# Partition sums of three adaLN column groups by selector products and one transpose, with an opening product group, GpSimd's work and one seed moved

## The chip, the cores and the metric

The kernel runs on one core of a Trainium2 chip. The core has TensorE (PE in the profile; its weight loads are PEld), VectorE (DVE), ScalarE (ACT), GpSimd (POOL) and SyncE (SP), which here issues nearly all loads of weights. The metric is the time of one execution on the device in microseconds (us), the median of several runs.

## The reference

One decoder block on 256 tokens of width 2048, in fp32. A conditioning vector c gives, by one large matrix `w_ada` (2048 x 12288), a shift, a scale and a gate for each of two sub-layers; two convolutional or attention parts and a gated feed-forward net use them.

```python
mod = jax.nn.silu(c) @ w_ada[l] + b_ada[l]
sh1, sc1, g1, sh2, sc2, g2 = jnp.split(mod, 6, axis=-1)
h = modulate(rms_norm(x, norm1_g[l]), sh1, sc1)          # h * (1 + scale) + shift
q, k, v, gb, gc, xt = split(h @ w_in[l])                 # 6 x 1024 columns
mixed = concat(rms_norm(attention(rms_norm(q), rms_norm(k), v)), rms_norm(gb * causal_dwconv(gc * xt)))
x = x + g1 * (mixed @ w_out[l])
h2 = modulate(rms_norm(x, norm2_g[l]), sh2, sc2)
u_gate, u_up = split(causal_dwconv(h2 @ w_ffn_up[l]))    # 2 x 5632 columns
x = x + g2 * ((silu(u_gate) * u_up) @ w_ffn_down[l])
```

The six parts of `mod` are numbered 0 to 5 in the kernel; part 3 is the second shift and part 4 the second scale, each 2048 wide, as 16 chunks of 128 columns.

## The kernel before

**Main products.** Every weight matrix is read once, in pieces of 128 x 1024 fp32 (tile `raw`, 10 buffers, loaded by SP in one order). A piece is split in two: ACT rounds it to `hi` (fp32r, L947), and DVE or GpSimd subtracts to get `lo` (L958); there are 6 buffers of each. PE then makes three fp32r products for each block (L1194 to L1196): activations with `hi`, with `lo`, and the activations' own rest with `hi`; in the feed-forward part the same three stand as L1545 and L1549. The groups of in-projection products are called `mq`, `mk`, `mv`, `mg`, `mc`, `mx` by the columns that they make; their partial sums `pa_q`, `pa_k` and so on are taken out of PSUM by ACT (L1214) or added up by DVE (L1216), or put back as the start of the next group by ACT (a "seed"). `h0` to `h15` are the normed input's 16 chunks; each takes a subtraction on DVE or GpSimd (L1631).

**Slots.** The program is a list of some 205 slots of 24 main products each: 49 for the in-projection, 16 for the out-projection (names `m('A', f)` and `m('C', f)`), then the feed-forward part. In a slot ACT makes the `hi` and DVE or GpSimd the `lo` of the slot two further on. A table, `CFG`, says by hand which `lo` GpSimd makes (`'pool'`: 1 or 2 for one half of a slot, 3 for both, 0 for none), which partial sums are seeds, where each small step stands (`'move'`, `'cls'`), how many buffers there are and in what order the opening runs (`'start'`). Each engine works through its own list in order, so what waits holds back all behind it.

**adaLN.** A group of columns of `w_ada` (class `Ada`) is either multiplied on PE in tiles of 32 columns (L1034, the conditioning vector repeated 32 times, so that sums come out 32-fold), or by DVE, one row block at a time (L1049, L1051). Both leave a 128-row tile (`adae` or `ada`) whose column sums over the 128 partitions are wanted. `cols()` gets them: for each chunk of 128 columns a transpose on PE (L1089, tile `adac`), for each four chunks one sum by DVE (L1091, tile `adaz`), then two or one small DVE steps (L1099, L1104, L1105) into the columns A2 and B2, by which the second norm's output is scaled and shifted (L1435 `h2f`, L1440 `h`). The last `ada` step of a group on DVE that accumulates in PSUM writes to SBUF (`adae`) and so lets the bank go; banks are handed out in turn, and the next user waits.

**Opening.** Before slot 2 the list `'start'` mixes transposes of x (`xn`, tokens `tr`), their copies (`out`), first `ada` groups, and the first products (`go slot piece`). `xn7` is the last of the transposes.

**Attention.** `att_t` transposes (L1726), ACT copies `qT`, `kT` (L1729, L1730), `as` are the score products (L1737). L1755 is an ACT step on 128 x 128 fp32 there. The norm before the feed-forward part ends in `n2d` (DVE, L1412), a product `n2b`, and `rB` on ACT (L1419).

Of the kernel before, what the change touches and what calls it, by code (L numbers as in the profile page):

```python
# [14 lines left out]
P = 128  # L15
# [22 lines left out]
       'bufs': [41, 14, 10, 6, 2],  # L38
# [23 lines left out]
               18: 2,  # L62
# [57 lines left out]
               93: 2,  # L120
# [92 lines left out]
               64: 6,  # L213
# [7 lines left out]
               84: 1,  # L221
               90: 0,
# [13 lines left out]
               109: 4,  # L236
               159: 2,
# [19 lines left out]
                18: 2,  # L257
# [27 lines left out]
                58: 1,  # L285
# [6 lines left out]
                65: 1,  # L292
                66: 3,
                68: 2,
                72: 0,
                83: 0},
       'pool_h': [4, 5, 6, 7, 8, 9, 10, 11, 15],
# [57 lines left out]
                 67: 3,  # L355
                 69: 4,
# [112 lines left out]
                 'evac_in q1 True': 3,  # L469
# [48 lines left out]
                'att_o 2': (0, 2),  # L518
# [24 lines left out]
                'att_t 3': (0, -2),  # L543
# [5 lines left out]
                'broadcast 5 2': (-1, 0),  # L549
# [31 lines left out]
                'evac 1 8': (2, 0),  # L581
                'evac 2 4': (1, 3),
# [8 lines left out]
                'evac_c 3 1': (0, 1),  # L591
# [52 lines left out]
                'qk_stat q1': (4, -3),  # L644
# [16 lines left out]
                'up_conv 1': (-1, 0.5),  # L661
                'up_conv 14': (0, -1),
# [46 lines left out]
       'seed': ['c0 3', 'c1 3', 'k1 3', 'x0 1', 'k0 3', 'v0 2', 'g0 1', 'g1 2', 'g1 1', 'g0 2'],  # L709
# [9 lines left out]
       'conv': [[1, 2, 2, 5, 4, 7, 7, 8], [2, 3, 2, 3, 2, 3, 2, 6]],  # L719
# [3 lines left out]
       'fcols': 14,  # L723
# [11 lines left out]
       'fused': [2, 3, 7, 8, 9, 12, 13],  # L735
# [3 lines left out]
       'sq': [3, 6, 0],  # L739
       'tr': [4, 7, 1],  # L740
       'part': -1,
       'up': [[1, 3], [1, 3], [0, 0], [2, 2]],
       'gate': [-21, -14, -2, -11],
# [36 lines left out]
               'evac_out': 1},  # L780
# [3 lines left out]
       'hi_late': [1, 2, 3, 5, 7, 8, 9, 10, 13, 14, 15, 17, 19, 20, 21, 25, 26, 27, 32, 33, 34, 40, 49, 50, 51, 52, 55, 56,  # L784
# [6 lines left out]
def tile_block(  # L791
# [194 lines left out]
    class Ada:  # L986


        def __init__(self, part, c0, n, pe, psum=False):
            self.part, self.c0, self.n, self.pe, self.psum = part, c0, n, pe, psum or pe  # L990
            self.rows = 2048 // n
            self.tiles = NK // self.rows
            self.nch = n // P
            self.w = min(n, 512 if self.psum else n)
            self.seen = 0
            self.out = False
            self.own = [] if [part, c0] in CFG["own"] else None

# [20 lines left out]

        def consume(self, r, part=None):  # L1020
            if r == 0 and part != 1:
                self.start()
            if part != 0:
                self.seen += 1
            size = 1024 if self.own is None else 512
            for j in range(self.rows) if part is None else range(8 * part, 8 * part + 8):
                i = self.rows * r + j
                x = j * self.n % size
                if x == 0:
                    h = take() if self.own is None else self.own.pop(0)  # L1030
                t, last = h[:, x:x + self.n], self.own is None and x + self.n == 1024
                if self.pe:
                    q = 32 * (j % 4)
                    mm(self.acc[0][q:q + 32, :], crep[:, i, :], t,  # L1034
                       start=(r == 0 and j < 4), stop=(r == self.tiles - 1 and j >= self.rows - 4),
                       tile_position=(0, q))
# [40 lines left out]
        def cols(self):  # L1077
# [3 lines left out]
            for a in range(0, self.nch, 4):  # L1081
# [10 lines left out]
                self.finish(z, self.c0 + a, m, scale)  # L1092

# [639 lines left out]
    def att_s(h):  # L1733
# [261 lines left out]
    def slot(i):  # L1995
# [22 lines left out]
        for g, r in extra.get(i, []):  # L2018
            g.consume(r)
# [107 lines left out]
```

## Time and profile before

| what | value |
|---|---|
| median of 3 runs | 1174.56 us (1174.26 to 1174.75) |
| profiled execution | 1173.49 us |
| its span (first to last instruction) | 1171.6 us |
| granted TensorE clock | 0.998 |
| PE busy | 1155.4 us, 99% |
| DVE / ACT / GpSimd busy | 917.6 / 646.9 / 169.3 us |
| read from memory | 314.87 MB, 272 GB/s over the span |

The profile is one execution. A row of a timeline has the start and length in us, the engine, the line, the instruction, its output and inputs with shape, a count where several alike follow each other, and in brackets the time that the engine stood idle before it and what ended that. A row of the chain of waits has start, length and what the end of the program was waiting for in that time. A row of the groups by line has busy time, mean ns of one, and idle time. A wait for several things is put down to the one that came last by the profile.

### The profile page before, as it was taken

The page shows a single profiled execution, that of the slowest core. Times are in us where ns is not written, and L with a number is a line of the kernel's source. Part 1 is how long each engine was busy: PE and PEld are TensorE (multiplying, and loading weights), DVE is VectorE, ACT ScalarE, POOL GpSimd, SP SyncE. Part 2 cuts the span into 40 slices and gives each one's busy share as a digit, 9 for nine tenths or more (in the row PEclk, how much of TensorE's full clock was granted, in tenths as well). Part 3 has the DMA queues.
Part 4 walks back from the last instruction along what each step waited for, and adds up shares of the span by engine and source line. Part 5 has one row for each costly group of instructions (what it writes and reads, how often), then busy time and mean ns, then how long its engine had stood idle before and what let it go on. Part 6 is the DMA issues. An engine that isn't in the chain of part 4 may idle for free.

```text
span 1171.6 us, 17108 instructions
## 1 busy us (share of the span) xinstructions
PE 1155.4 (99%) x5989; PEld 965.8 (82%) x5989; DVE 917.6 (78%) x1311; ACT 646.9 (55%) x1002; POOL 169.3 (14%) x100
## 2 busy tenths in 40 slices
PE   7999999999999999999999999999999999999998
PEld 5678888878777878888888888888888888888886
DVE  4469979997788989999999544768888897666785
ACT  4666565578566455556676444555435554445461
POOL 0768673631001021000000000000000000000000
PEclk9999999999999999999999999999999999999999
DMA  9999999995799989986465755576887877875541
GB/s 349 405 405 374 406 353 386 390 388 170 262 368 315 362 272 360 378 276 208 156 207 187 235 180 181 175 230 220 284 299 262 306 245 231 292 246 174 169 155 72
DMA packets 205382, 320.22 MB, mean 273 GB/s; under 512 B 13816, under 2 KB 112300, under 8 KB 205296
## 3 DMA queue, kind: packets, MB, share of 16 engines
q1 hardware_dynamic: 202336, 314.68, 77.2%
q10 hardware_dynamic: 2352, 4.22, 1.3%
q8 instruction: 47, 0.77, 0.3%
q14 instruction: 39, 0.32, 0.1%
q0 software_dynamic: 608, 0.23, 0.1%
HBM read 314.87 MB, written 4.21 MB: 272 GB/s over the span
## 4 chain that ended last, share of the span: by engine, by line
PE 91%; DMA 5%; DVE 3%; issue 1%; ACT 0%; POOL 0%; SPq 0%; DVEq 0%; POOLq 0%; ACTq 0%
PE z L1545 27%; PE z L1549 14%; DMA raw<-in_w_in_dram 2%; DMA raw<-in_w_ada_dram 2%; PE ada L1034 1%; PE mx L1194 1%; PE mx L1196 1%; PE mx L1195 1%; PE mk L1194 1%; DVE ada L1051 1%; PE mg L1194 1%; PE mg L1196 1%; PE mc L1194 1%; PE mq L1194 1%; PE mc L1196 1%; PE mg L1195 1%
## 5 line engine op out<-in xcount | busy, mean ns | idle before, releaser
L947 ACT ACTIVATE hi<-raw 128x1024 fp32r<-128x1024 f32 (+1 forms) x401 | 401.2, 1030 | 314.2 <-PE z L1545 92.9
L958 DVE TENSOR_TENSOR lo<-raw,hi 128x1024 fp32r<-128x1024 f32 x340 | 397.6, 1208 | 95.6 <-ACT hi L947 90.3
L1545 PE MATMUL z<-h,hi 128*128 128x512 f32 x1408 | 328.9, 390 | 0.0
L1545 PEld LDWEIGHTS z<-h,hi 128*128 128x128 f32 x1408 | 261.3, 188 | 52.6 <-DVE h L1440 0.3
L1051 DVE SCALAR_TENSOR_TENSOR ada<-raw,csil,ada 128x512 f32<-128x512 f32 (+2 forms) x215 | 189.0, 892 | 5.6 <-DMA raw<-in_w_ada_dram 2.0
L958 POOL TENSOR_TENSOR lo<-raw,hi 128x1024 fp32r<-128x1024 f32 x61 | 150.5, 2489 | 269.2 <-ACT hi L947 269.2
L1549 PEld LDWEIGHTS z<-h,lo 128*128 128x128 f32 x1408 | 174.8, 192 | 3.4
L1549 PE MATMUL z<-h,lo 128*128 128x256 f32 x1408 | 176.0, 283 | 0.0
L1110 POOL MEMSET gb<- 128x512 f32 x2 | 1.1, 526 | 491.8 <-DVE uy L1484 491.8
L1461 DVE TENSOR_TENSOR ub<-z,ub 128x256 f32<-128x256 f32 x120 | 43.8, 417 | 34.5 <-ACT ub L1458 34.4
L1458 ACT ACTIVATE ub<-z 128x256 f32<-128x256 f32 x120 | 39.7, 383 | 31.1 <-PE z L1545 31.0
L1477 ACT ACTIVATE uy<-ub,vcols 128x256 f32<-128x256 f32 x88 | 45.6, 593 | 6.8 <-DMA gr<-gs 6.7
L1482 DVE SCALAR_TENSOR_TENSOR uy<-ub,vcols,uy 128x255 f32<-128x255 f32 x88 | 42.1, 479 | 5.7 <-ACT uy L1477 5.6
L1484 DVE SCALAR_TENSOR_TENSOR uy<-ub,vcols,uy 128x254 f32<-128x254 f32 x88 | 42.5, 483 | 3.1
L1493 ACT ACTIVATE gh<-uy 128x512 fp32r<-128x512 f32 x22 | 13.9, 630 | 40.6 <-DVE uy L1491 40.6
L1487 ACT ACTIVATE uy<-uy 128x512 f32<-128x512 f32 x22 | 13.9, 633 | 37.2 <-DVE uy L1484 37.2
L1034 PE MATMUL ada<-raw,crep 128*32 128x512 f32 (+1 forms) x224 | 27.1, 525 | 3.2 <-DMA raw<-in_w_ada_dram 2.7
L1494 DVE TENSOR_TENSOR gl<-uy,gh 128x512 fp32r<-128x512 f32 x22 | 15.2, 693 | 17.9 <-ACT gh L1493 17.9
L1194 PE MATMUL mk<-hi,h 128*128 128x512 f32 x64 | 25.8, 403 | 0.0
L1194 PE MATMUL mq<-hi,h 128*128 128x512 f32 x64 | 25.3, 395 | 0.4 <-ACT pa_g L1214 0.4
L1194 PE MATMUL mg<-hi,h 128*128 128x512 f32 x64 | 25.7, 401 | 0.0
L1194 PE MATMUL mx<-hi,h 128*128 128x512 f32 x64 | 25.3, 396 | 0.0
(574 smaller groups left out, 1922.8 us busy)
## 6 DMA issues: line engine op xcount, KB each, us to landing
raw<-in_w_ada_dram SPq DMA_DIRECT2D x180, 512.0 KB, 6.8
raw<-in_w_ffn_up_dram SPq DMA_DIRECT2D x352, 256.0 KB, 4.7
raw<-in_w_in_dram SPq DMA_DIRECT2D x95, 512.0 KB, 7.1
raw<-in_w_ffn_down_dram SPq DMA_DIRECT2D x76, 512.0 KB, 4.7
raw<-in_w_out_dram SPq DMA_DIRECT2D x32, 512.0 KB, 6.1
raw<-in_w_ada_dram SPq DMA_DIRECT2D x24, 256.0 KB, 6.6
raw<-in_w_ffn_down_dram SPq DMA_DIRECT2D x24, 256.0 KB, 3.8
xr<-in_x_dram SPq DMA_DIRECT2D x4, 512.0 KB, 5.4
```

What stands on the lines that cost most here:

```text
L947: act(piece(his, "hi")[:, :m], t[:, :m], AF.Copy)
L958: (nc.gpsimd if pool in (i + 1, 3) else V).tensor_tensor(out=piece(los, "lo")[:, :m], in0=t[:, :m], in1=hi[:, :m].bitcast(F32), op=ALU.sub ...
L1034: mm(self.acc[0][q:q + 32, :], crep[:, i, :], t, start=(r == 0 and j < 4), stop=(r == self.tiles - 1 and j >= self.rows - 4), tile_positio ...
L1051: V.scalar_tensor_tensor(out=self.acc[n], in0=v, scalar=csil[:, i:i + 1], in1=acc, op0=ALU.mult, op1=ALU.add)
L1194: mm(o, a, hi[k], start=(first and k == 0 and not seeded), stop=False, skip_group_check=True)
L1458: act(c[ft // 2][:, (ft % 2) * 256:(ft % 2) * 256 + 256], zp[grp][ft][:, 256:], AF.Copy)
L1461: V.tensor_tensor(out=d, in0=zp[grp][ft][:, :256], in1=d, op=ALU.add)
L1477: act(y, b, AF.Identity, bias=fcols[3][:, i:i + 1], scale=fcols[2][:, i:i + 1])
L1482: V.scalar_tensor_tensor(out=y[:, 1:], in0=b[:, :255], scalar=fcols[1][:, i:i + 1], in1=y[:, 1:], op0=ALU.mult, op1=ALU.add)
L1484: V.scalar_tensor_tensor(out=y[:, 2:], in0=b[:, :254], scalar=fcols[0][:, i:i + 1], in1=y[:, 2:], op0=ALU.mult, op1=ALU.add)
L1545: mm(zp[grp][ft], blk(hi, j)[:, ft * P:(ft + 1) * P], h2T[k + j], start=k + j == ks[0], stop=k + j == ks[1] - 1)
L1549: mm(zp[grp][ft][:, :256], blk(lo, j)[:, ft * P:(ft + 1) * P], h2T[k + j][:, :256], start=False, stop=False)
```

## The change

**The sums of groups (3, 0), (3, 4) and (4, 0)**, 16 chunks together, are no longer made by `cols()`. A new step `cols_set` does them at once, two slots after the last of the three groups. A selector tile `pick` is zero but for one column of ones (or 1/32, for groups from PE); a window of 32 of its columns starting at 7 - n has that column at place n. With it as weights a product in a 32-column tile puts the sums of one chunk over partitions into row 32 q + n of one bank, and adds to the rest; four chunks stand side by side, n counts the groups of four. ACT copies the 128 x 128 result (`adar`), PE transposes it once (`adat`), and the small DVE steps read their columns from that bank.

**The opening**: `go 1 2` (six products of slot 1 with `h1`) stands ahead of `xn7` and of the `ada` batches.

**GpSimd**: `lo` of slots 18, 25, 26, 27, 29, 58, 65 and 66 go to DVE in whole or half; one half each of slots 117 to 124 and 187 to 189, and both of 153 and 200, come to GpSimd. The subtractions of `h2` and `h14` go from DVE to GpSimd.

**Seeds**: `k0 3` and `g0 2` are no longer started from a seed (DVE adds their partial sums instead, and ACT need not empty `mg` at 162 us), `k1 2` is.

Smaller: group (3, 0) takes its data one slot later (`'lag'`), the vector columns come two slots later, one more 2 KB buffer, `c32` has 32 columns, other entries of the tables for single steps. The branch `'ttr'` is off. The diff, cut:

```diff
-       'bufs': [41, 14, 10, 6, 2],
+       'bufs': [42, 14, 10, 6, 2],
...
                 16: 3,
                 17: 3,
-                18: 2,
+                18: 0,
...
-                25: 3,
-                26: 3,
-                27: 2,
+                25: 0,
+                26: 0,
+                27: 0,
                 28: 0,
-                29: 3,
+                29: 0,
...
+                117: 1,
...
+                153: 3,
...
+                200: 3},
-       'pool_h': [4, 5, 6, 7, 8, 9, 10, 11, 15],
+       'pool_h': [2, 4, 5, 6, 7, 8, 9, 10, 11, 14, 15],
...
-       'seed': ['c0 3', 'c1 3', 'k1 3', 'x0 1', 'k0 3', 'v0 2', 'g0 1', 'g1 2', 'g1 1', 'g0 2'],
+       'seed': ['c0 3', 'c1 3', 'k1 3', 'x0 1', 'v0 2', 'g0 1', 'g1 2', 'g1 1', 'k1 2'],
...
-       'fcols': 14,
+       'fcols': 16,
...
-                 'tr 4', 'go 0 2', 'out 4', 'out 5', 'tr 6', 'out 6', 'tr 7', 'out 7', 'slot 0', 'slot 1', 'go 1 2'],
+                 'tr 4', 'go 0 2', 'out 4', 'out 5', 'tr 6', 'go 1 2', 'out 6', 'tr 7', 'out 7', 'slot 0', 'slot 1'],
...
+       'lag': {'3 0': 1},
+       'sets': [[[3, 0], [3, 4], [4, 0]]],
+       'ttr': False}
...
-    c32 = const.tile([P, P], F32, name="c32")
+    c32 = const.tile([P, 32], F32, name="c32")
     nc.vector.memset(c32, 1.0 / 32.0)
+    pick = {}
+    for v in (1.0, 1.0 / 32.0):
+        if CFG["sets"]:
+            pick[v] = const.tile([P, 39], F32, name=f"pick{int(1 / v)}")
+            nc.gpsimd.memset(pick[v], 0.0)
+            nc.gpsimd.memset(pick[v][:, 7:8], v)
...
+        def cols_set(self):
+            groups = self.set
+            p = bank(f"adas{self.part}_{self.c0}", full=False)
+            parts = [(g, a) for g in groups for a in range(0, g.nch, 4)]
+            for n, (g, a) in enumerate(parts):
+                assert g.out
+                flush(g)
+                e = pick[1.0 / 32.0 if g.pe else 1.0][:, 7 - n:39 - n]
+                m = min(4, g.nch - a)
+                for q in range(m):
+                    mm(p[32 * q:32 * q + 32, :P], e, g.chunk(a + q), start=n == 0, stop=n == len(parts) - 1,
+                       tile_position=(0, 32 * q))
+            r = t1k("adar")[:, :P]
+            act(r, p[:, :P], AF.Copy)
+            p = bank(f"adat{self.part}_{self.c0}", full=False)
+            nc.tensor.transpose(p[:, :P], r, ident)
+            for n, (g, a) in enumerate(parts):
+                m = min(4, g.nch - a)
+                g.finish(p[:, n:n + 32 * m - 31:32], g.c0 + a, m, 1.0)
```

How the instructions move is seen in each engine's own order. PE in the opening, before (`xn` are transposes of x, `ada` the first groups, h_333 is `h1` and h_308 `h0`):

```order
L2029 MATMUL xn_413<-ident,xr 128x128 x4
L2029 MATMUL xn_420<-ident,xr 128x128 x4
L1034 MATMUL ada_2_0_439<-raw_199,crep 32x256 x2
...
L1034 MATMUL ada_2_0_439<-raw_240,crep 32x256 x2
L1194 MATMUL mk_401<-hi,h_333 128x512
...
L1196 MATMUL mk_402<-hi,h_333 128x512
L1194 MATMUL mc_501<-hi,h_308 128x512
```

and after, with other tile numbers (h_339 is `h1`, h_314 `h0`):

```order
L2120 MATMUL xn_419<-ident,xr 128x128 x4
L1249 MATMUL mk_407<-hi,h_339 128x512
...
L1251 MATMUL mk_408<-hi,h_339 128x512
L2120 MATMUL xn_432<-ident,xr 128x128 x4
L1069 MATMUL ada_2_0_451<-raw_205,crep 32x256 x2
...
L1069 MATMUL ada_2_0_451<-raw_246,crep 32x256 x2
L1249 MATMUL mc_507<-hi,h_314 128x512
```

The six `mk` with `h1` now stand ahead of the last `xn` and of the `ada` batches; `mc` follows `ada` at once.

PE at the sums: before, the transposes of group (4, 0) in the out-projection:

```order
L1196 MATMUL m('A', 3)1_4126<-hi,mix_2765 128x512
L1089 MATMUL adac_0_4189<-ident,ada_0_3038 128x128 x4
L1089 MATMUL adac_0_4198<-ident,ada_0_3038 128x128 x4
L1194 MATMUL m('A', 3)0_4125<-hi,mix_3059 128x512
L1195 MATMUL m('A', 3)0_4125<-lo,mix_3059 128x512
```

and after, the whole set, between two chunks of `m('C', 2)`, some 11 us earlier in the program:

```order
L1251 MATMUL m('C', 2)1_4026<-hi,mix_3454 128x512
L1139 MATMUL adas_0_4051<-ada_0_3042,pick_79 32x128 x8
L1139 MATMUL adas_0_4051<-adae_0_3640,pick_82 32x128 x4
L1139 MATMUL adas_0_4051<-adae_4_3642,pick_82 32x128 x4
L1144 MATMUL adat_0_4070<-ident,adar 128x128
L1249 MATMUL m('C', 2)0_4025<-hi,mix_3630 128x512
```

The other two groups' transposes (four each, at 353 and 359 us) are gone from their places too. The transpose stands right behind the selector products that it depends on by way of ACT's `adar`.

DVE between two additions to `pa_q` in the in-projection, before (170 to 185 us):

```order
L1216 TENSOR_TENSOR pa_q_487<-mq_1756,pa_q_487 128x512
L1051 SCALAR_TENSOR_TENSOR ada_0_0_1781<-raw,csil,ada_0_0_1781 128x512
...
L958 TENSOR_TENSOR lo<-raw,hi 128x1024
L1216 TENSOR_TENSOR pa_k_653<-mk_1849,pa_k_653 128x512
L1216 TENSOR_TENSOR pa_k_655<-mk_1850,pa_k_655 128x512
L1051 SCALAR_TENSOR_TENSOR ada_0_0_1781<-raw,csil,ada_0_0_1781 128x512
...
L958 TENSOR_TENSOR lo<-raw,hi 128x1024 x2
```

and after:

```order
L987 TENSOR_TENSOR lo<-raw,hi 128x1024 x2
L1271 TENSOR_TENSOR pa_q_491<-mq_1759,pa_q_491 128x512
L1271 TENSOR_TENSOR pa_q_493<-mq_1760,pa_q_493 128x512
L1086 SCALAR_TENSOR_TENSOR ada_0_0_1785<-raw,csil,ada_0_0_1785 128x512
...
L987 TENSOR_TENSOR lo<-raw,hi 128x1024 x2
L1086 SCALAR_TENSOR_TENSOR ada_0_0_1785<-raw,csil,ada_0_0_1785 128x512
...
L987 TENSOR_TENSOR lo<-raw,hi 128x1024 x4
L1271 TENSOR_TENSOR pa_k_486<-mk_1949,pa_k_486 128x512
L1271 TENSOR_TENSOR pa_k_488<-mk_1950,pa_k_488 128x512
```

More `lo` stand on DVE here, in groups of two and four, and another pair of `pa_k` is added up (k0 where k1 was); over the whole stretch up to the `pa_q` at 205.83 us there are 16 `lo` in place of 9.

More of the change, by code (lines that the diff above doesn't have):

```diff
@@ L236 @@
                109: 4,
+               114: 0,
+               148: 2,
                159: 2,
@@ L291 @@
                 64: 0,
-                65: 1,
-                66: 3,
+                65: 0,
+                66: 1,
                 68: 2,
                 72: 0,
-                83: 0},
-       'pool_h': [4, 5, 6, 7, 8, 9, 10, 11, 15],
+                83: 0,
+                117: 1,
+                118: 1,
+                119: 1,
+                120: 1,
+                121: 1,
+                122: 1,
+                123: 1,
+                124: 1,
+                153: 3,
+                187: 1,
+                188: 1,
+                189: 1,
+                200: 3},
+       'pool_h': [2, 4, 5, 6, 7, 8, 9, 10, 11, 14, 15],
        'psum': [[0, 45]],
@@ L1018, in start, with hold @@
                 self.acc = [(t4k if self.n > 512 else t2k)(what)[:, :self.n]]
+        def hold(self, r):
+            tiles = self.rows * self.n // (1024 if self.own is None else 512)
+            self.held[r] = [take() if self.own is None else self.own.pop(0) for _ in range(tiles)]
         def consume(self, r, part=None):
@@ L1029, in consume @@
                 if x == 0:
-                    h = take() if self.own is None else self.own.pop(0)
+                    src = self.held.get(r, self.own)
+                    h = take() if src is None else src.pop(0)
                 t, last = h[:, x:x + self.n], self.own is None and x + self.n == 1024
@@ L1598, in tile_block, with in_set @@
     ready_at = {}
+    held_until = {}
+    sets = {(part, c0): n for n, e in enumerate(CFG["sets"]) for part, c0 in e}
+    filling = {}
+    def in_set(g, s):
+        n = sets.get((g.part, g.c0))
+        if n is None:
+            return False
+        filling.setdefault(n, []).append((s, g))
+        if len(filling[n]) < len(CFG["sets"][n]):
+            return True
+        s, gs = max(s for s, _ in filling[n]), [g for _, g in filling[n]]
+        gs[0].set = gs
+        at(s + 2, gs[0].cols_set)
+        ready_at.update({(g.part, g.c0 + k): s + 2 for g in gs for k in range(g.nch)})
+        return True
     def spread_loads(g, a, span):
@@ L1604, in spread_loads @@
             extra.setdefault(s, []).append((g, r))
+            lag = CFG["lag"].get(f"{g.part} {g.c0}", 0)
+            if lag:
+                s += lag
+                held_until.setdefault(s, []).append((g, r))
         at(s + 1, g.evac)
+        if in_set(g, s):
+            return
         if g.gate():
@@ L1739, in att_s @@
         s = t2k("s")[:, :384]
-        V.tensor_tensor(out=s, in0=p[:, :384], in1=mask, op=ALU.add)
         m, z = small(2, "m"), small(2, "z")
-        V.reduce_max(out=m[:, 0:1], in_=s[:, :128], axis=AX.X)
-        V.reduce_max(out=m[:, 1:2], in_=s[:, 128:], axis=AX.X)
+        if CFG["ttr"]:
+            for t, a, b in ((0, 0, 128), (1, 128, 384)):
+                V.tensor_tensor_reduce(out=s[:, a:b], in0=p[:, a:b], in1=mask[:, a:b], scale=1.0, scalar=NEG,
+                                       op0=ALU.add, op1=ALU.max, accum_out=m[:, t:t + 1])
+        else:
+            V.tensor_tensor(out=s, in0=p[:, :384], in1=mask, op=ALU.add)
+            V.reduce_max(out=m[:, 0:1], in_=s[:, :128], axis=AX.X)
+            V.reduce_max(out=m[:, 1:2], in_=s[:, 128:], axis=AX.X)
         i, j = (col("q", t, h) for t in range(2))
@@ L2018, in slot @@
         for g, r in extra.get(i, []):
+            if f"{g.part} {g.c0}" in CFG["lag"] and (g, r) not in fill:
+                g.hold(r)
+            else:
+                g.consume(r)
+        for g, r in held_until.get(i, []):
             g.consume(r)
```

45 lines of the change are left out of this document (26 added, 19 removed), and 7 rows, old and new, of tables.

## The prediction

> **What bounds the kernel now.** I read the page first, then the chain of waits by stage, then the timelines of single engines at each place where TensorE (PE) stands still.
>
> ```profile
> PE 1155.4 (99%) x5989; PEld 965.8 (82%) x5989; DVE 917.6 (78%) x1311; ACT 646.9 (55%) x1002; POOL 169.3 (14%) x100
> PE 91%; DMA 5%; DVE 3%; issue 1%; ACT 0%; POOL 0%; SPq 0%; DVEq 0%; POOLq 0%; ACTq 0%
> L958 DVE TENSOR_TENSOR lo<-raw,hi 128x1024 fp32r<-128x1024 f32 x340 | 397.6, 1208 | 95.6 <-ACT hi L947 90.3
> L958 POOL TENSOR_TENSOR lo<-raw,hi 128x1024 fp32r<-128x1024 f32 x61 | 150.5, 2489 | 269.2 <-ACT hi L947 269.2
> ```
>
> PE is busy 99% of the span and makes 91% of the chain that ended last, and the change leaves the main products as they are. So time can come only from PE instructions that go or shrink, or from the few places where PE waits. Three such places lie near the change. The first is in the opening (the timeline of PE; columns are start, length, instruction, and idle time before it with what ended it):
>
> ```profile
> 33.96 1.07 PE L1034 MATMUL ada<-raw,crep 128*32 128x256 f32 x16 [0.25 <-ACT xnT L2037]
> 36.66 3.14 PE L1034 MATMUL ada<-raw,crep 128*32 128x256 f32 x16 [1.63 <-DMA raw<-in_w_ada_dram]
> 39.73 0.80 PE L1194 MATMUL mk<-hi,h 128*128 128x512 f32 x1
> 41.55 0.40 PE L1194 MATMUL mc<-hi,h 128*128 128x512 f32 x1
> ```
>
> The second batch of `ada` starts when its data land, and takes 3.14 us where the first, of the same size, takes 1.07: it waits inside too. The six products `mk` then run 39.73 to 41.55, 1.82 us. The second place is in the chain of waits around 162:
>
> ```profile
> 151.92 8.49 DMA raw<-in_w_in_dram
> 160.79 0.97 ACT hi L947
> 161.77 0.58 ACT pa_g L1214
> 162.39 0.50 PE mq L1194
> 162.89 0.23 PE mq L1195
> ```
>
> `mq` waits for ACT to empty the bank of `mg` (`pa_g`), and ACT is busy with a `hi` whose transfer came late. The third is the first attention product:
>
> ```profile
> 250.25 0.47 ACT L1730 ACTIVATE kT<-at,vcols 128x256 f32<-128x256 f32 x1
> 252.23 0.46 PE L1737 MATMUL as<-kT,qT 128*128 128x128 f32 x2 [0.87 <-ACT kT L1730]
> 251.33 0.75 DVE L1051 SCALAR_TENSOR_TENSOR adae<-raw,csil,ada 128x512 f32<-128x512 f32 x1
> ```
>
> The view names `kT`, but the first `kT` ended at 250.72. The bank that `as` takes is the one that DVE's last `ada` step reads, and that ends at 252.08: DVE, not ACT, lets PE go. So what counts at 251 is when DVE is through.
>
> **The opening.** The six `mk` move ahead of `xn7` and of both `ada` batches. The second batch still ends with its data, at about 39.7, and `mc` follows it at once in place of at 41.55. What moves is 6 products; in a run of products each adds 0.23 (the last row of the chain above), 6 x 0.23 = 1.4, up to the whole 1.82. In front they push the first `ada` batch from 33.96 to about 35.4; it then ends at 36.5, before 36.66, so the wait for DMA covers them. Without that wait the move would be worth nothing. I take a gain of 1.4, bounds 0 and 1.8.
>
> **At 162.** The seed moves: `g0`'s bank is now emptied by two DVE adds and `mq` no longer queues behind ACT's `pa_g`. What is late next is DVE's own step before them:
>
> ```profile
> 159.15 0.75 DVE L1051 SCALAR_TENSOR_TENSOR adae<-raw,csil,ada 128x512 f32<-128x512 f32 x1
> 168.04 1.28 DVE L1216 TENSOR_TENSOR pa_q<-mq,pa_q 128x512 f32<-128x512 f32 x2
> 174.21 2.72 DVE L1051 SCALAR_TENSOR_TENSOR ada<-raw,csil,ada 128x512 f32<-128x512 f32 x4
> 176.84 3.17 DVE L958 TENSOR_TENSOR lo<-raw,hi 128x1024 fp32r<-128x1024 f32 x1
> 183.76 2.35 DVE L958 TENSOR_TENSOR lo<-raw,hi 128x1024 fp32r<-128x1024 f32 x2
> 190.35 4.45 DVE L958 TENSOR_TENSOR lo<-raw,hi 128x1024 fp32r<-128x1024 f32 x2 [1.60 <-ACT hi L947]
> 205.83 1.37 DVE L1216 TENSOR_TENSOR pa_q<-mq,pa_q 128x512 f32<-128x512 f32 x2 [1.17 <-PE mq L1196]
> 231.19 2.89 DVE L958 TENSOR_TENSOR lo<-raw,hi 128x1024 fp32r<-128x1024 f32 x1 [1.33 <-ACT hi L947]
> 169.43 12.85 POOL L958 TENSOR_TENSOR lo<-raw,hi 128x1024 fp32r<-128x1024 f32 x5
> 187.82 4.76 POOL L958 TENSOR_TENSOR lo<-raw,hi 128x1024 fp32r<-128x1024 f32 x2 [5.54 <-ACT hi L947]
> ```
>
> `adae` ends at 159.90; with the transposes that read it `mq` can start at about 160.5 in place of 162.39. So PE is 1.4 ahead until there and 1.9 ahead behind it.
>
> **162 to 252, DVE's load.** The 7 GpSimd `lo` at 169 to 193 (the last two rows) go to DVE. They stand behind the `pa_q` of 168.04 in DVE's order, so idle time before it takes none of them. That `pa_q` comes about 2.0 earlier (167.3 end in place of 169.3, as `mq` is 1.9 earlier and one `h` subtract leaves DVE). From there to 205.83 DVE now has 36.5 us, of which 0.96 (172), 1.60 and 1.17 are idle (the first is in the row below; behind it the table by stretches: length, busy time of PE, its weight loads, DVE, ACT and GpSimd, granted clock, DMA share, GB/s):
>
> ```profile
> 172.92 1.37 DVE L1216 TENSOR_TENSOR pa_q<-mq,pa_q 128x512 f32<-128x512 f32 x2 [0.96 <-PE mq L1196]
> 170.00:180.00 10.00, 10.00 (x46) 8.29 (x45) 9.04 (x11) 2.74 (x4) 10.00 (x5) 1.00 0.79 257
> 210.00:220.00 10.00, 10.00 (x46) 8.29 (x45) 9.89 (x15) 3.90 (x6) 5.15 (x3) 1.00 1.05 407
> ```
>
> So 32.8 us of work. Added: 7 x 1.18 (183.76: 2.35 for two) = 8.3. Taken away: beside GpSimd's five, one DVE `lo` took 3.17 in place of 1.2, and beside its two, a pair took 4.45 in place of 2.35; with GpSimd silent that returns 2.0 + 2.1 = 4.1. The `pa_k` adds only change places (k0 in, k1 out). 32.8 + 8.3 - 4.1 = 37.0, from 167.3: `pa_q` at 204.3 with no idle at all, and 206.4 with two microseconds of it. I take 0.6 of idle, 204.9, 0.9 earlier than now, since DVE's three present waits shrink when it has more to do. Behind that DVE is full (9.89 of 10 at 210 to 220) up to 231.19, where its wait of 1.33 ends on a `hi`, that is on DMA. The stretch 170 to 180 moved 257 GB/s where 210 to 220 moved 407; GpSimd was busy in all of it, and a raw buffer is only free when its `lo` is done. That dip is worth 10 x (1 - 257/407) = 3.7 us of transfers, and with half of it filled the `hi` comes early enough. So `as` comes 0.9 earlier, and PE, which is there 1.9 earlier, waits 1.0 longer than now. Bounds for `as`: 0 (DMA no earlier) and 1.9 (no longer wait than now).
>
> **The set of sums.** The rows for what is removed and added are in the timeline of PE, the chain, and the groups by line:
>
> ```profile
> 352.93 0.66 PE L1089 MATMUL adac<-ident,adae 128*128 128x128 f32 x4
> 409.74 1.03 PE L1089 MATMUL adac<-ident,ada 128*128 128x128 f32 x8
> 150.07 0.45 PE adac L1089 x4
> 150.54 0.71 DVE adaz L1091
> 351.93 1.06 PE L1034 MATMUL ada<-raw,crep 128*32 128x512 f32 x8
> L1755 ACT ACTIVATE s<-s,r 128x128 f32<-128x128 f32 x8 | 3.2, 396 | 1.1 <-DVE r L1754 1.0
> 410.53 0.48 PE L1194 MATMUL m('A', 3)0_4125<-hi,mix 128*128 128x512 f32 x1
> 353.34 0.48 PE L1194 MATMUL m('A', 1)0_3515<-hi,mix 128*128 128x512 f32 x1
> ```
>
> Removed: the first four take 352.93 to 353.34, 0.41; the second four stand alone, 0.45 as in the chain row, and 0.09 because the first product behind such a group is longer (0.48 against the 0.39 to 0.40 of `mc`); the eight take 409.74 to 410.53, 0.79, and the same 0.09. Together 1.83. Added: 16 fp32 products of 128 columns, four column tiles side by side. In the trace a product of this kind is two rows. The `ada` batch of 8 rows at 512 columns starts 1.00 before what follows it, two rounds of four, so a round at 128 columns is about 1.00 / 2 / 4 = 0.12, and 32 rows are 8 rounds, 0.95. Then PE waits: the last product ends 0.25 behind the point where the next could start (0.66 against 0.41 in the first row), its reader starts 0.02 later (150.07 + 0.45 to 150.54), ACT's 128x128 copy is 0.40, the transpose 0.11, a switch 0.09. Sum 1.82, so net 0.0. In PE's order nothing stands between the last selector product and the transpose, so this wait of some 0.7 is open; on ACT the copy is queued behind two `hi` whose data should be there, and two `y` and the next `hi` behind it come later, which no one near is waiting for. Bounds: -0.4 (the wait is 0.3) and +1.0 (ACT is still in a `hi`, 0.97 at 160.79). DVE loses four reductions of 0.71 and gains none; PE does not feel it.
>
> The Trainium skill's Perfetto Trace Analysis, Optimizing Tensor Performance, Transposes, speaks against this edit: a logical transpose should be a transpose and not a standard product, since transposes skip arithmetic. No trace here has the selector product; if each took a transpose's 0.11 for itself, the set would cost 0.8 more and the sum would come to 1174.5. The rows of `ada`, which are standard products in column tiles, speak for the smaller figure.
>
> **The rest.** GpSimd gets 15 `lo` in FFN slots: 2.49 each in place of 1.21, made two slots (2 x 24 x 0.23 = 11 us) ahead of PE, which is the cover; nothing. The clearing of the selector tiles, the narrower constant, one more buffer, the vector columns two slots later: nothing. One edit has no cover: DVE now does a `lo` between the norm's `n2d` and `h2f`:
>
> ```profile
> 431.14 0.48 DVE L1412 TENSOR_SCALAR n2d<-ident,n2r 128x128 f32<-128x128 f32 x2
> 432.83 0.87 DVE L1435 SCALAR_TENSOR_TENSOR h2f<-x1T,A,n2b 128x256 f32<-128x256 f32 x2 [1.21 <-ACT rB L1419]
> 434.43 0.50 PE L1545 MATMUL z<-h,hi 128*128 128x512 f32 x1
> ```
>
> Its gap is 1.21, the `lo` 1.2: it fits to the tenth; at 3.17 it would cost 1.9. I take 0.
>
> **The sum.** Opening and 162 give 1.9 at PE, of which 0.9 pass `as`; set 0.0; rest 0. The profiled execution took 1173.49 (span 1171.6 and 1.9 around it); it becomes 1172.6. The median of the runs is 1174.56, 1.07 above the profiled one, so the median after is 1173.7. What a measurement can tell from no change here is about 0.2%, 2.35 us: below 1172.2 is faster, above 1176.9 slower.
>
> **Rivals.** (a) All of it passes: DVE is through 2.5 to 2.8 earlier, so most of the 0.87 that PE now waits before `as` goes as well, and the set may give its 0.4: 1.4 + 0.5 + 0.6 to 0.9 + 0 to 0.4 = 2.5 to 3.2, about 1171.7. For it: with the 231.19 `lo` at 1.2 another 1.7 is there. Against: DVE has almost no idle left to give up, and the row of 231.19 ends on a transfer. The skill's SBUF — State Buffer, SBUF: two separate sides, would favour it: GpSimd and a DVE instruction with two SBUF inputs hold a shared port one at a time, the other blocked for the whole instruction. The trace agrees for `lo` (3.17 and 4.45) but not for the `ada` steps, which have two such inputs and take 0.68 each from 174.21 on, beside GpSimd. Chance 0.32.
>
> (b) Slower: the moved `lo` overload DVE. If the 4.1 do not come back (the `lo` rows were slow for another reason) and 2 us of waits for `hi` stay, DVE needs 32.8 + 8.3 + 2 = 43.1 from 167.3: `pa_q` at 210.4, 4.6 late; the 1.33 at 231 takes up some, `as` is 3.3 late: about 1177.8. It decides from `pa_q` later than 207.2 on, and costs 2.35 from 209.5 on. For it: DVE at 9.04 to 9.89 of 10. Against: GpSimd's rows overlap just those two slow ones. Chance 0.14.
>
> (c) It does nothing: DMA keeps `hi` at 231 where it is, and `as` stays at 252.2: 1174.5. Chance 0.10. My own case has 0.44, with its own range 1172.6 to 1174.6.
>
> **Numbers.** Faster: nearly all of (a) and a little of mine, 0.34. Slower: most of (b), 0.12. The rest, 0.54, within 0.2%. The range that leaves out 2 in 10 runs from the far end of (a), 1171.4, less the 0.4 by which the opening may bring 1.8, so 1171.0, to where slower begins, 1176.9; most of (b) lies outside.
>
> **What would show it.** `mc` first at 39.7 to 40.2; `mq` of 162.39 at about 160.5, by DVE; no DVE `lo` over 2 us between 170 and 195; `pa_q` of 205.83 at 204.3 to 206; `as` at 251.3 with a wait of 1.9 before it; 1.8 from the first selector product to the next main product; `z` 0.9 earlier than 434.43. The forecast is wrong if `as` is before 250 (a) or after 254 (b), or if the set costs over 2.8.

## The result: slower, because the transfers of the weights land 64 bytes lower

The changed kernel took 1179.93 us (median of 6 runs, 1177.99 to 1183.78) beside 1174.47 us for the kernel before in the same session; the ratio is 1.0052, with an interval of 1.0034 to 1.0069. The forecast was 1173.7 with a range to 1176.9: the change is slower, and outside the range. The execution profiled after took 1178.84 (span 1177.1).

The page of the kernel after: the engines' busy times, the chain that ended last, and the GB/s in 40 equal slices.

```profile
PE 1157.4 (98%) x6006; PEld 965.1 (82%) x6006; DVE 922.2 (78%) x1303; ACT 645.5 (55%) x997; POOL 181.9 (15%) x110
PE 93%; DMA 4%; DVE 2%; ACT 0%; SPq 0%; issue 0%; ACTq 0%
GB/s 333 381 383 384 386 389 385 385 379 179 254 334 359 333 260 373 366 300 211 179 182 203 232 172 193 160 229 217 302 283 268 308 244 253 258 255 180 170 153 72
```

The same row of the kernel before:

```profile
GB/s 349 405 405 374 406 353 386 390 388 170 262 368 315 362 272 360 378 276 208 156 207 187 235 180 181 175 230 220 284 299 262 306 245 231 292 246 174 169 155 72
```

Engines and chain look alike. What differs is the start of the last row: before, three of the first five slices stand at 405 or 406; after, no slice is above 389. The table by stretches shows it for 110 to 150, where PE does the same work and the DMA engines are full in both (columns as in the prediction; the last two are the DMA share and GB/s). Before, then after:

```profile
110.00:150.00 40.00, 40.00 (x185) 33.05 (x184) 38.77 (x54) 22.88 (x31) 26.98 (x16) 1.00 1.05 407
```

```profile
110.00:150.00 40.00, 40.00 (x185) 33.12 (x184) 38.55 (x55) 22.87 (x32) 22.07 (x13) 1.00 1.04 385
```

Nearly the same share of busy time moves 385 in place of 407 GB/s, 5% less. The first nine slices, 29 us each and so up to 265 us, are those in which the kernel takes all that the transfers give; there it costs time. The timeline of PE after:

```profile
39.25 2.83 PE L1069 MATMUL ada<-raw,crep 128*32 128x256 f32 x16 [1.43 <-DMA raw<-in_w_ada_dram]
42.01 0.50 PE L1249 MATMUL mc<-hi,h 128*128 128x512 f32 x1
55.70 0.50 PE L1249 MATMUL mk<-hi,h 128*128 128x512 f32 x1 [1.42 <-ACT pa_x L1269]
57.99 2.19 PE L1069 MATMUL ada<-raw,crep 128*32 128x512 f32 x8
60.31 0.48 PE L1249 MATMUL mv<-hi,h 128*128 128x512 f32 x1
256.57 0.46 PE L1818 MATMUL as<-kT,qT 128*128 128x128 f32 x2 [2.25 <-DVE adae L1086]
439.88 1.40 PE L1600 MATMUL z<-h,hi 128*128 128x512 f32 x5
```

`mc` comes at 42.01 where it came at 41.55. Then `mk` waits 1.42, the `ada` batch at 57.99 takes 2.19 where it took 1.09 before, and `mv` is 3.6 late (60.31 against 56.72). `as` is 4.3 later than 252.23, its own wait being 1.4 longer (2.25 against 0.87); `z` is 5.5 later than 434.43, and the span ends 5.5 later (1177.1 against 1171.6). So most of the loss is there by 60 us, and behind `as` only about 1 us more is lost.

**Where the 64 bytes come from.** Tiles stand in SBUF behind one another in the order in which they are made. `c32` shrinks from 128 to 32 columns, 384 bytes less on each partition; the two `pick` tiles of 39 columns have 156 bytes each and take up 160, 320 more. So `hi`, `lo`, `raw` and all that follows moves 64 bytes down. Before, each raw buffer starts at a multiple of 512 bytes in its partition (77312 for the first, then steps of 4096); after, at 77248, 448 past one. The theory to be tested was then: the start of a transfer's destination sets its rate. The rivals: the selector products, GpSimd's moved work or the opening are slow in themselves.

### The profile page after: what moved, and what is told of

Same layout as the page of the kernel before. It is cut to its first block, busy times and chain, and to the rows that moved or that the text cites. A ratio compares the mean times of both kernels' runs of the same rounds, so it can differ in the third digit from the quotient of the medians.

```text
span 1177.1 us, 17164 instructions
## 1 busy us (share of the span) xinstructions
PE 1157.4 (98%) x6006; PEld 965.1 (82%) x6006; DVE 922.2 (78%) x1303; ACT 645.5 (55%) x997; POOL 181.9 (15%) x110
## 4 chain that ended last, share of the span: by engine, by line
PE 93%; DMA 4%; DVE 2%; ACT 0%; SPq 0%; issue 0%; ACTq 0%
PE z L1600 27%; PE z L1604 14%; DMA raw<-in_w_ada_dram 3%; PE mg L1249 1%; PE mg L1251 1%; PE mg L1250 1%; PE ada L1069 1%; PE mx L1249 1%; PE mk L1249 1%; PE mv L1249 1%; PE mx L1251 1%; PE mv L1251 1%; PE mv L1250 1%; PE mq L1251 1%; PE mk L1250 1%; PE mk L1251 1%
## 5 line engine op out<-in xcount | busy, mean ns | idle before, releaser
L987 DVE TENSOR_TENSOR lo<-raw,hi 128x1024 fp32r<-128x1024 f32 (+1 forms) x336 | 397.1, 1217 | 101.2 <-ACT hi L976 93.1
L987 POOL TENSOR_TENSOR lo<-raw,hi 128x1024 fp32r<-128x1024 f32 (+1 forms) x65 | 160.5, 2491 | 926.0 <-ACT hi L976 897.5
L1086 DVE SCALAR_TENSOR_TENSOR ada<-raw,csil,ada 128x512 f32<-128x512 f32 (+2 forms) x215 | 193.0, 910 | 5.7 <-DMA raw<-in_w_ada_dram 2.1
L1069 PE MATMUL ada<-raw,crep 128*32 128x512 f32 (+1 forms) x224 | 30.2, 527 | 3.5 <-DMA raw<-in_w_ada_dram 2.6
L1249 PE MATMUL mc<-hi,h 128*128 128x512 f32 x64 | 25.4, 397 | 0.0
```

What stands on the lines that cost most here:

```text
L987: (nc.gpsimd if pool in (i + 1, 3) else V).tensor_tensor(out=piece(los, "lo")[:, :m], in0=t[:, :m], in1=hi[:, :m].bitcast(F32), op=ALU.sub ...
L1069: mm(self.acc[0][q:q + 32, :], crep[:, i, :], t, start=(r == 0 and j < 4), stop=(r == self.tiles - 1 and j >= self.rows - 4), tile_positio ...
L1086: V.scalar_tensor_tensor(out=self.acc[n], in0=v, scalar=csil[:, i:i + 1], in1=acc, op0=ALU.mult, op1=ALU.add)
L1249: mm(o, a, hi[k], start=(first and k == 0 and not seeded), stop=False, skip_group_check=True)
```

## Experiments

Every kernel below that computes the block was timed beside the kernel before on the same chip.

**1. The change with the old starts.** One number is changed, so that the pick tiles take 384 bytes:

```diff
-            pick[v] = const.tile([P, 39], F32, name=f"pick{int(1 / v)}")
+            pick[v] = const.tile([P, 48], F32, name=f"pick{int(1 / v)}")
```

> The changed kernel, its two selector tiles 48 columns wide in place of 39, so that all tiles behind them lie 64 bytes further on and the raw buffers start at multiples of 512 bytes of a partition again, as before the change; nothing else moves. Theory A (placement: the change moved the raw buffers to 448 above a multiple of 512, and transfers into them run some 5% slower): the stretches 110 to 150 move 405 GB/s again in place of 377 to 388, and the time falls from 1179.9 to 1171.4 to 1174.6, what the forecast gave for the edits alone. Theory B (the order: lo on DVE, the moved seed, the set): 377 to 388 GB/s and about 1179 as with 39 columns.

Measured: 1173.29 us beside 1173.64, ratio 0.9996 (0.9987 to 1.0005). The whole loss is gone, and no gain is left that could be told from none. Its instructions are those of the kernel after, but for two clearings that are nine columns wider. Its stretch 110 to 150:

```profile
110.00:150.00 40.00, 40.00 (x186) 33.07 (x185) 38.90 (x53) 21.57 (x30) 24.94 (x14) 1.00 1.04 395
```

That is less than the 405 expected: 369 GB/s from 120 to 130, where the DMA share falls to 1.01, and 398 to 407 in the other three tens of it. In the kernel after, no ten of this stretch moves more than 388.

**2 to 4. The kernel before with other starts.** Only the width of `c32` is changed; no instruction uses more than its first 32 columns.

```diff
-    c32 = const.tile([P, P], F32, name="c32")
+    c32 = const.tile([P, 112], F32, name="c32")
```

> The kernel before, with the constant c32 112 columns wide in place of 128: only the tiles behind it move, 64 bytes down, so that the raw buffers start at 448 above a multiple of 512 bytes. Theory A: 385 GB/s at 110 to 150 in place of 406, and slower than before by 3 to 8 us, 1177 to 1182. Theory B: 406 GB/s and 1174.5, within 1 us.

> The kernel before, with c32 96 columns wide: the raw buffers start at 384 above a multiple of 512 bytes (128 down). Theory A says that a start which is no multiple of some block costs; if the block is 128 or 64 bytes, this runs as before (406 GB/s, 1174.5), if it is 256 or 512, as the shift by 64 (385 GB/s, 1177 to 1182). Theory B: 1174.5.

> The kernel before, with c32 64 columns wide: the raw buffers start at 256 above a multiple of 512 bytes. Theory A with a block of 512 bytes: 385 GB/s and 1177 to 1182; with 256 or less: 406 GB/s and 1174.5. Theory B: 1174.5.

Measured (the raw buffers' start past a multiple of 512 in brackets): 112 columns (448) 1181.12, ratio 1.0062 (1.0050 to 1.0075); 96 columns (384) 1180.22, 1.0060 (1.0046 to 1.0073), with 387 GB/s from 110 to 150; 64 columns (256) 1173.63, 1.0004 (0.9994 to 1.0013). The stretch 110 to 150 with 112 and with 64 columns:

```profile
110.00:150.00 40.00, 40.00 (x185) 33.08 (x185) 39.05 (x54) 22.80 (x32) 25.15 (x14) 1.00 1.05 386
```

```profile
110.00:150.00 40.00, 40.00 (x185) 33.01 (x185) 38.87 (x54) 22.84 (x31) 28.63 (x16) 1.00 1.05 406
```

The unchanged program loses as much as the changed one did once its buffers are moved, and nothing at 256: of the starts tried here, those that are a multiple of 256 are the fast ones.

**5. Transfers alone.** A kernel that only loads (one execution): seven groups of 48 transfers of 512 KB, whose destinations start 0, 64, 128, 256, 192, 32 and 0 bytes past a multiple of 256, in this order.

> Only loads, the block's computation is left out (x is copied to the output): 7 groups of 48 loads of 512 KB from w_in, rows of 2 KB as in the kernel, into ten buffers in turn; DVE reads one column of each. The groups (tiles raw0x to raw6x) start 0, 64, 128, 256, 192, 32 and again 0 bytes above a multiple of 256. Theory A: groups 0, 3 and 6 at one rate, the others some 5% lower, no other engine being at work. If the loads alone do not show it, it takes the kernel's other traffic, and rival A2 or a mixture stands. At 405 GB/s a group of 25.2 MB takes 62 us, at 385 it takes 65.

Its table by stretches, one row inside each group (columns: stretch, length, busy time of DVE and GpSimd, granted clock, DMA share, GB/s):

```profile
20.00:60.00 40.00, 4.76 (x31) 0.00 (x0) 1.00 1.05 407
80.00:120.00 40.00, 4.46 (x29) 0.00 (x0) 1.00 1.05 387
145.00:185.00 40.00, 4.45 (x29) 0.00 (x0) 1.00 1.05 387
215.00:250.00 35.00, 4.10 (x27) 0.00 (x0) 1.00 1.05 407
270.00:310.00 40.00, 4.46 (x29) 0.00 (x0) 1.00 1.05 387
340.00:380.00 40.00, 4.61 (x30) 0.00 (x0) 1.00 1.05 387
412.00:440.00 28.00, 3.22 (x21) 0.00 (x0) 1.00 1.05 408
```

407 or 408 GB/s at 0 and 256, 387 at 32, 64, 128 and 192: 5% less, as in the kernels, with nothing computed beside it and no matter how far off the start is. The Trainium skill's DMA: Bandwidth & Descriptors, How a descriptor splits into AXI transactions, says, of what a transaction reads, that it must start at a multiple of 256 bytes, and that the first transaction of a descriptor that starts elsewhere begins at the multiple below it, so that the bytes between are fetched for nothing. The block of 256 agrees with the runs, in which it is the destination that is off. The Trainium skill's count of beats in that section grows with the distance (an estimate from it for a piece of 2 KB: 65 beats in place of 64 for 32 bytes off, 70 for 192); the runs show one cost for all four, so the measurement decides, and how the 5% arise is left open.

**6. A gap ahead of the raw buffers.** The kernel before, with an unused 64-byte tile between `lo` and `raw`:

```diff
+    gap = sb.tile([P, 16], F32, tag="gap", bufs=1, name="gap")
+    nc.gpsimd.memset(gap, 0.0)
     for _ in range(N_RAW):
         load_next()
```

> The kernel before, with an unused tile of 64 bytes put between the lo buffers and the raw buffers: constants, hi and lo stay where they were, the raw buffers and all behind them start 64 bytes above a multiple of 512. Theory A (what costs is where transfers land): 385 GB/s at 110 to 150 and 1177 to 1182. Rival A2 (what costs is that engines read and write hi and lo at a shifted start, and the loads only follow): 406 GB/s and 1173.6.

Measured: 1189.81, ratio 1.0124 (1.0100 to 1.0147). 110 to 150 moves 384 GB/s, as Theory A has it, but the time is not the 1177 to 1182 expected: it is twice the loss of experiment 2, and a product of `mq` takes 396 ns there in place of 389. The gap moves two things, the raw buffers and, behind them, the activations `h` and `mix`, which PE multiplies with `hi` and `lo`; `hi` and `lo` stay. The next two kernels part them: `raw` alone (64 bytes ahead of it, 192 behind it, so that the activations are at a multiple of 256 again), and the activations alone (64 bytes behind `raw`; with them move the other tiles behind it, among them those of the shorter transfers).

> Before with an unused tile of 64 bytes ahead of the raw buffers and one of 192 bytes behind them: the raw buffers start 64 bytes past a multiple of 256, and all tiles behind them (the activations h and mix, the shorter transfers) start at multiples of 256 again. Theory: the start of a transfer's destination sets its rate, and the extra loss of the run with the gap alone came from activations that no longer start at a multiple of 256 as hi and lo do: 384 to 388 GB/s from 110 to 150 us, products of mq at 389 ns, 1179 to 1182 us. Rival: a raw buffer at 64 is worse than one at 128 or 192 and slows the products too: products of 395 ns and 1187 to 1191 us.

> Before with an unused tile of 64 bytes behind the raw buffers: hi, lo and the raw buffers start where they did, the activations and the shorter transfers behind them 64 bytes later. Theory: the transfers into raw keep 404 to 408 GB/s from 110 to 150 us, and the products, whose activations now start 64 bytes past a multiple of 256, take 395 ns in place of 389; 6 ns on each of some 1600 products between 70 and 440 us are 9.6 us, some of it hidden by waits that then fall away: 1177 to 1184 us. Rival: the products stay at 389 ns (the gap alone slowed them by its raw buffers) and the time is that of before: 1173.5 to 1175.

Measured: `raw` alone 1179.93, ratio 1.0054 (1.0036 to 1.0072); activations alone 1185.80, ratio 1.0101 (1.0087 to 1.0115), a little above the 1177 to 1184 expected. The stretch 110 to 150 and the products of `mq` in it (count, busy time, mean ns), for `raw` alone:

```profile
110.00:150.00 40.00, 40.00 (x185) 33.09 (x184) 38.98 (x53) 20.90 (x29) 27.23 (x15) 1.00 1.04 385
```

```profile
L1194 PE MATMUL mq<-hi,h 128*128 128x512 f32 x16 | 6.2, 389 | 0.0
```

and for the activations alone:

```profile
110.00:150.00 40.00, 40.00 (x181) 32.27 (x180) 38.94 (x54) 22.15 (x30) 27.55 (x15) 1.00 1.05 404
```

```profile
L1194 PE MATMUL mq<-hi,h 128*128 128x512 f32 x16 | 6.3, 394 | 0.0
```

Two effects, each by itself: `raw` off by 64 bytes slows the transfers (385 GB/s) with `hi` and `lo` where they were, which rules out rival A2, and leaves the products at 389 ns; activations off by 64 bytes against `hi` and `lo` leave the transfers (404) and lengthen the products of the in-projection to 394 ns, with 181 matmul instructions in 40 us in place of 185. In the feed-forward part it is mixed: `z` with `hi` takes 392 ns in place of 390, `z` with `lo` 278 in place of 283. In the changed kernel `hi`, `lo` and the activations moved together, and its 185 instructions and 389 ns for `mq` show that only the first effect is at work there.

**7. The parts of the change, with the old starts.** Each kernel is that of experiment 1 with one part undone: the `lag` of group (3, 0); the opening; GpSimd's slots 18 to 29; the selector products (in whose place the sixteen transposes and four reductions of before stand again; the expectation words them otherwise).

```diff
-       'lag': {'3 0': 1},
+       'lag': {},
```

> The changed kernel with its raw buffers at multiples of 512 (as e1_after_pad) and without the entry that lets group (3, 0) take its data one slot after they were claimed. In e1_after_pad PE waits about 1.0 inside an ada batch at 333 us for a transfer that it did not wait for before. Theory: the claimed buffers stay occupied one slot longer and push the next loads back; without the entry the batch takes 1.9 in place of 2.9, and the time is about 1.0 below e1_after_pad, 1172.3. Rival: the batch only stands earlier against the same transfer (PE is 1.1 ahead there) and the wait stays: 1173.3.

```diff
-                 'tr 4', 'go 0 2', 'out 4', 'out 5', 'tr 6', 'go 1 2', 'out 6', 'tr 7', 'out 7', 'slot 0', 'slot 1'],
+                 'tr 4', 'go 0 2', 'out 4', 'out 5', 'tr 6', 'out 6', 'tr 7', 'out 7', 'slot 0', 'slot 1', 'go 1 2'],
```

> The changed kernel at multiples of 512 (as e1_after_pad) with the six mk products back behind slot 1, as before. In e1_after_pad mc starts 1.95 earlier than before, but at 56.6 (mv behind the ada batch of 55) only 0.1 is left. Theory (the batch of 55 waits for its transfer, which does not come earlier, so the opening gives nothing): mc at 41.5, mv at 56.6 to 56.8, mq of 161.48 within 0.3, and the time within 0.5 of e1_after_pad, 1173.3. Rival (my forecast: the 1.4 survive to 160): mq 1.4 later, as later by up to 0.9, 1174.2.

```diff
-                 18: 0,
+                 18: 2,
...
-                 25: 0,
-                 26: 0,
-                 27: 0,
+                 25: 3,
+                 26: 3,
+                 27: 2,
...
-                 29: 0,
+                 29: 3,
```

> The change with its pick tiles 48 columns wide (raw buffers at the starts of before), and GpSimd's steps of the slots 18, 25, 26, 27 and 29 given back as before (2, 3, 3, 2 and 3); nothing else is undone. Theory: the moved steps are what brings as forward (251.26 with the whole change, 252.23 in before), so as comes at 252.0 to 252.3 again, with DVE's pa_q at 205.5 to 206.0; but the step is given away again at the next wait for ada (2.92 against 1.92), so the time is that of the whole change within 0.3 us: 1173.0 to 1174.3. Rival: the 1.0 us at as reaches the end: 0.8 to 1.2 us slower than the whole change with aligned buffers. Second rival: as comes at 251.3 all the same, since it is the opening that moved it.

```diff
-       'sets': [[[3, 0], [3, 4], [4, 0]]],
+       'sets': [],
...
-    c32 = const.tile([P, 32], F32, name="c32")
+    c32 = const.tile([P, P], F32, name="c32")
```

> The change without its selector products: the three groups are summed by the four products and four transposes each of before, the constant is 128 columns wide as in before, so that the raw buffers start where they did; the opening, GpSimd's steps and the seed are as changed. Theory: the sixteen selector products, copy and transpose take 1.56 us where the removed products and transposes took 1.83, so this kernel is 0.0 to 0.4 us slower than the whole change with aligned buffers: 1173.0 to 1174.3, with as at 251.2 to 251.5. Rival: the set costs more than it saves (a wait of the transpose for ACT's copy, 0.40, and a wait of the products behind it): this kernel is 0.5 to 1.0 us faster than the whole change with aligned buffers.

Measured, as ratios to the kernel before: without `lag` 0.9993 (0.9981 to 1.0004); opening as before 0.9991 (0.9980 to 1.0001); GpSimd as before 1.0010 (0.9997 to 1.0022); without the selector products 1.0005 (0.9996 to 1.0013). Against experiment 1's 0.9996 (0.9987 to 1.0005) none is told apart by time. The traces, one execution each, tell more:

- **Without `lag`** the batch, now at 334.95, takes 1.92 again, as expected, but the time is not 1.0 lower and `z` comes at 434.62. A batch of 8 `ada` products stands at 318.84 again; `lag` moves it to the batch of 350. So the wait goes and no gain comes.
- **Opening as before**: `mc` at 40.76 (41.5 was expected), `mv` at 56.90, `mq` at 161.81 in place of 161.48, `as` at 251.36 in place of 251.26. From `mv` on the opening is worth 0.1 to 0.3 in these traces.
- **GpSimd as before**: `as` at 252.17, in the range expected; `pa_q` at 204.59, earlier than the 205.5 expected. This execution was a long one, 1176.46 beside a median of 1174.13.

```profile
252.17 0.46 PE L1818 MATMUL as<-kT,qT 128*128 128x128 f32 x2 [2.05 <-DVE adae L1086]
```

- **Without the selector products**: `as` at 251.35, as expected, and a span of 1172.4 against 1171.4. The sign is the one expected, but the difference is no larger than executions of one kernel differ.

`as` comes at 251.26 to 251.79 in the four traces with the `lo` moved, and at 252.17 to 252.31 in the three aligned ones without (GpSimd as before, the kernel before, and its shift by 256). So the moved `lo` bring `as` forward, and the opening does not. Whether that 0.9 reaches the end is not settled by time: the ratios differ by 0.0014, or 1.6 us, but their intervals overlap, and the two kernels ran on different chips.

## Why the prediction was wrong

**The step that failed** is in the part on the rest: "The clearing of the selector tiles, the narrower constant, one more buffer, the vector columns two slots later: nothing." The cost of the narrower constant and of the selector tiles was looked for in instructions, and they have none to speak of; what they cost is the place where they put everything behind them: 5.7 us of span (1177.1 after, 1171.4 with the same instructions at the old starts). Experiments 1 to 5 and `raw` alone in experiment 6 show this. The sum's other terms can only be judged at the old starts, so on the kernel of experiment 1. Its timeline of PE:

```profile
39.60 0.50 PE L1249 MATMUL mc<-hi,h 128*128 128x512 f32 x1 [0.45 <-ACT pa_q L1269]
52.39 0.50 PE L1249 MATMUL mk<-hi,h 128*128 128x512 f32 x1 [0.70 <-ACT pa_x L1269]
54.66 1.81 PE L1069 MATMUL ada<-raw,crep 128*32 128x512 f32 x8
56.60 0.48 PE L1249 MATMUL mv<-hi,h 128*128 128x512 f32 x1
161.12 0.60 PE L1124 MATMUL adac<-ident,adae 128*128 128x128 f32 x4
251.26 0.46 PE L1818 MATMUL as<-kT,qT 128*128 128x128 f32 x2 [1.08 <-DVE adae L1086]
333.25 2.92 PE L1069 MATMUL ada<-raw,crep 128*32 128x512 f32 x16
350.41 1.92 PE L1069 MATMUL ada<-raw,crep 128*32 128x512 f32 x16
434.27 3.90 PE L1600 MATMUL z<-h,hi 128*128 128x512 f32 x16
```

Three more rows of the kernel before, to hold these against:

```profile
56.72 0.49 PE L1194 MATMUL mv<-hi,h 128*128 128x512 f32 x1
319.28 1.07 PE L1034 MATMUL ada<-raw,crep 128*32 128x512 f32 x8
335.38 1.92 PE L1034 MATMUL ada<-raw,crep 128*32 128x512 f32 x16
```

- **Opening, 1.4 carried to 162: wrong.** `mc` starts 1.95 earlier (39.60 against 41.55; the upper bound was 1.8), of which 1.2 are the opening's (40.76 with it undone), close to the 1.4. But `mk` then waits for ACT and the next `ada` batch takes 1.81 where it took 1.09 before: `mv` behind it is only 0.12 earlier. The cover of the step, data that come late anyway, is there a second time 15 us on, and I did not look. The run with the opening undone agrees: `as` at 251.36.
- **At 162, `mq` at 160.5: half right.** The wait for ACT is gone, but PE is not 1.4 ahead when it comes there: the transposes that stand ahead of `mq` start at 161.12, and `mq` at 161.48, 0.9 earlier where 1.9 was forecast.
- **162 to 252, `as` 0.9 earlier: right in size**, 0.97 (251.26 against 252.23), and by GpSimd's steps, as experiment 7 shows; the way to it only in part. The wait ahead of `as` is 1.08 and not 1.9, since PE is less far ahead. DVE's rows, and the stretch that moved 257 GB/s before:

```profile
167.27 1.28 DVE L1271 TENSOR_TENSOR pa_q<-mq,pa_q 128x512 f32<-128x512 f32 x2
168.47 3.00 DVE L987 TENSOR_TENSOR lo<-raw,hi 128x1024 fp32r<-128x1024 f32 x2
189.93 4.62 DVE L987 TENSOR_TENSOR lo<-raw,hi 128x1024 fp32r<-128x1024 f32 x4
205.47 1.28 DVE L1271 TENSOR_TENSOR pa_q<-mq,pa_q 128x512 f32<-128x512 f32 x2
230.18 2.39 DVE L987 TENSOR_TENSOR lo<-raw,hi 128x1024 fp32r<-128x1024 f32 x1 [0.93 <-ACT hi L976]
250.37 0.75 DVE L1086 SCALAR_TENSOR_TENSOR adae<-raw,csil,ada 128x512 f32<-128x512 f32 x1
```

```profile
170.00:180.00 10.00, 10.00 (x46) 8.27 (x45) 10.00 (x13) 6.30 (x9) 0.38 (x1) 1.00 1.04 409
```

  With GpSimd silent a `lo` takes 1.16 (4.62 for four), as taken; the pair at 168.47, 1.50 each, runs beside GpSimd's subtractions of `h` (168.95 to 170.39). `pa_q` is 0.4 earlier in place of 0.9, and still `as` has its 0.97: the dip is filled (409 GB/s), the `lo` of 231.19 gets its `hi` 1.0 earlier (230.18), and the last `adae` is through at 251.12 in place of 252.08. With GpSimd's old work `pa_q` is earlier still (204.59), yet that `lo` starts at 231.05. So it is the transfers that decide here, as the prediction says of the dip, and not the reckoning of `pa_q`.
- **Set of sums, net 0.0: nearly right.** From the first selector product to the next product it takes 1.56; with 0.09 for the longer product behind it 1.65, where 1.82 was summed and 1.83 is removed:

```profile
397.82 0.64 PE L1139 MATMUL adas<-ada,pick 128*32 128x128 f32 x16
398.28 0.62 PE L1139 MATMUL adas<-adae,pick 128*32 128x128 f32 x16
399.30 0.33 PE L1144 MATMUL adat<-ident,adar 128*128 128x128 f32 x1 [0.40 <-ACT adar L1142]
399.38 0.48 PE L1249 MATMUL m('C', 2)0_4025<-hi,mix 128*128 128x512 f32 x1
```

  Sixteen products in 32 rows, the last one's end included, take 399.30 - 0.40 - 397.82 = 1.08, where 0.95 + 0.25 was summed (8 rounds of 1.00 / 2 / 4 would be 1.00), and the wait for ACT's copy is 0.40. So 0.2 is gained. The Trainium skill's Perfetto Trace Analysis, Optimizing Tensor Performance, Transposes, wants a transpose where one is meant; the 0.8 more that the prediction set down for that case do not show in these rows, where sixteen products take 1.08 and not 16 x 0.11 = 1.76. They also sum over the partitions, which a transpose does not.
- **What passes to the end, 0.9: wrong by the trace.** The time cannot tell (0.9 us is a ratio of 0.9992, within experiment 1's interval), but `z` is 0.16 earlier, not 0.9: the `ada` batch of 333.25 takes 2.92 in place of 1.92. PE is 2.13 ahead there (333.25 against 335.38), of which some 1.0 is the batch of 8 that `lag` moves from 319.28 to the one of 350.41 (16 in place of 8) and that has yet to be done. The batch's weight loads, which it cannot go without, wait 0.86 for data:

```profile
334.26 0.16 PEld L1069 LDWEIGHTS ada<-raw,crep 128*32 128x32 f32 x8 [0.86 <-DMA raw<-in_w_ada_dram]
```

  So the 0.97 from `as` is given back at the next wait for a transfer, and what `z` has left is about the 0.2 of the set. That `lag` undone removes this wait and brings no gain (experiment 7) is not explained.
- **DVE's `lo` between `n2d` and `h2f`: right**, 1.22 long, and `n2b` comes at 431.52 in place of 431.68.
- **Rival (a)** did not come: `as` is at 251.26, not before 250. One of its arguments was misread. The `ada` steps beside GpSimd at 174.21 do not have two inputs from SBUF: their accumulator `ada` is a bank of PSUM (`bank(...)` in `Ada.start`), so that only `raw` is such a tile, and their 0.68 each are no exception to the rule that the prediction names.
- **Rival (b)** named the symptom, `pa_q` past 207.2 and `as` late: after, `pa_q` is at 209.42 and `as` 4.3 late. Its mechanism, an overloaded DVE, is refuted: the same DVE work at the old starts has `pa_q` at 205.47. That its time, 1177.8, came near the measured 1179.93 was luck.
- **Rival (c)**, that it does nothing, gives the time of experiment 1 as well as any (ratio 0.9996), but not by its reason: `as` did move.

## What to carry to other kernels

Where a kernel waits for its transfers, the address of their buffers is part of the kernel: a constant that shrinks or a new small tile ahead of them can cost more than the edit is worth. Keep such buffers at multiples of 256 bytes by a size that is a multiple of it, or by padding, and compare the GB/s of several full stretches with those of the kernel before, ahead of looking at any engine; one stretch alone can mislead (395 GB/s in experiment 1, which lost nothing). Here a gain ahead of a wait for data counted only up to the next such wait.

## What was unexpected of the hardware

- Transfers of 512 KB, in pieces of 2 KB, whose destination in SBUF does not start at a multiple of 256 bytes run at 387 GB/s in place of 407 to 408, the same for 32, 64, 128 and 192 bytes off.
- Products of the in-projection whose activations start 64 bytes off against their weights, `hi` and `lo`, take 394 ns in place of 389, with 181 matmul instructions in 40 us in place of 185. If both are moved by 64 bytes nothing is seen (389 ns at 448 past a multiple of 512). Other distances were not tried, and what makes it is open.
